# Start bytes of split weights and activations in their SBUF buffers, and two instead of three attention scratch buffers

## The chip, the cores and the metric

The kernel runs on one core of one Trainium2 chip. The metric is the device time of one execution in microseconds (us), as a median over runs. Engines are named as in the profile: PE is TensorE's matmul, PEld its weight load, DVE is VectorE, ACT is ScalarE, POOL is GpSimd, and SP issues DMAs.

## The reference

One decoder layer on 256 tokens of width 2048, all in float32:

```python
h = rmsnorm(x, ln1)
proj = h @ w_in                                   # 2048 x 6144
dq, dk, dv, sq, sk, sv = split(proj)              # six blocks of 1024 columns
diff_out = rmsnorm(differential_attention(rotary(dq), rotary(dk), dv, lam), diff_head_norm) * (1 - lam_init)
sb_out = rmsnorm(stick_breaking_attention(sq, sk, sv), sb_head_norm)
x = x + concat(diff_out, sb_out) @ w_out          # 2048 x 2048
h = rmsnorm(x, ln2)
x = x + square(relu(h @ w_mlp_in)) @ w_mlp_out    # 2048 x 8192, 8192 x 2048
return rmsnorm(x, ln_f)
```

## The kernel before

**Three passes.** Each large product is made of three passes in float32r, a 4-byte type: a value is split into H, its float32r rounding, and L, the rest, and x.w is taken as xH.wH + xH.wL + xL.wH, summed in PSUM.

**The weight stream.** Weights come by DMA in chunks of 512 rows by 512 columns (`w`, 1 MB). A chunk is used in two jobs of `HK` = 2 contraction tiles each. For a job ACT rounds half a chunk to `wh` (L214), DVE subtracts and writes `wl` (L217), both 128 x 1024 elements, which is 4,096 bytes in each partition, and PE multiplies. The conversions run 3 jobs ahead of PE, 5 in the MLP. `wh` and `wl` lie in the pool `spool`, 4 buffers each. In the MLP part every third job takes its pair from another pool, `mlp_split`, with 2 buffers each.

**The two shapes of product.** `products_acc` (L258, L259, L260) keeps activations stationary and streams weights: a matmul of 512 columns for each of xH.wH, xH.wL, xL.wH, and 12 to a job. It serves the projections dq, dk, dv, sv (`acc_..`), the output projection (`oacc`) and the second MLP product (`ma`). `products_T` (L272, L274) keeps weights stationary and streams activations: one matmul of 512 columns with wH against [xH | xL], one of 256 columns with wL against xH, 8 such pairs to a job. It serves sq, sk (`acc_sq`, `acc_sk`) and the first MLP product (`ia`). Every matmul loads a stationary operand of 128 columns (512 bytes a partition) ahead of it. Both operands are read from SBUF.

**Activations.** Split activations lie in the pool `apool` under one tag, `act`: 16 buffers of 4,096 bytes, in turn `xs`, `mixT`, `xs2` and `aT`, each [2 contraction tiles][H, L][256 tokens].

**Where the tiles begin.** In the program as built, the four `wh` buffers begin at byte 69,600 of each partition and every 4,096 after it, the `wl` buffers at 85,984, the `act` buffers at 102,368, the `mlp_split` buffers at 209,504. So all operands of these matmuls begin at 96 modulo 128. Take as *distance* the start of the stationary operand that is loaded for the next matmul minus the start of the present matmul's moving operand, modulo 512: with weights from `spool` it is 0 throughout, with weights from `mlp_split` it is 384 (L258 to L260) or 128 (L272, L274). 2,961 of the 3,920 matmuls of 512 float32r columns have distance 0.

**Attention** is written as generators that put a few instructions at a time between the jobs (`side`, `tick`). Its scratch tag `e` has three buffers: `e_d` of a differential head (L463 to L482), `t_s` and `a_s` of a pair of stick-breaking heads. PE, ACT and DVE run in the order in which the code is written; SP's loads are issued when a chunk has been converted.

Of the kernel before, what the change touches and what calls it, by code (L numbers as in the profile page):

```python
# [10 lines left out]
F32 = mybir.dt.float32  # L11
F32R = mybir.dt.float32r
BF16 = mybir.dt.bfloat16
# [3 lines left out]
PSUM = bass.MemoryType.PSUM  # L17

P = 128
S = 256  # L20
D = 2048
DFF = 4 * D
NT = S // P          # token tiles
KT = D // P          # contraction tiles of the model width
NB = 512             # columns of a weight block
CK = 4               # contraction tiles of one weight load
HK = 2               # contraction tiles of one split step
HG = 4               # heads of one column block
# [5 lines left out]
LN_IN = 2.0 ** -32                    # the Ln table ends at 2^64  # L34
LN_OUT = -16.0 * math.log(2.0)
LAM_INIT = 0.8 - 0.6 * math.exp(-0.3 * 0)
W_BUFS = 3           # weight loads in flight
S_BUFS = 4           # split steps in flight
START_ORDER = "x0 c0 x1 c1 m0 x2 c2 m1 c3 x3 m2 x4 c4 m3 c5 x5 m4 x6 c6 m5 c7 x7 m6"
WARM0, WARM1 = 5, 4  # products of zeros before and after the first transposes  # L40
AHEAD = 3            # split steps ahead of the products
# [3 lines left out]
def tile_hybrid_layer(  # L45
# [19 lines left out]
    """Every large product runs as three float32r passes: with x = H + L, H = float32r(x),  # L65
    x.w = xH.wH + xH.wL + xL.wH, all summed in float32 PSUM."""
# [9 lines left out]
    # ---------------------------------------------------------------- loads  # L76
# [16 lines left out]
    # ---------------------------------------------------------------- constants  # L93
    idle = cpool.tile([P, NB], BF16, name="idle")
# [13 lines left out]
    negtri = cpool.tile([P, P], F32, name="negtri")      # [l, j] = -1 where l >= j  # L108
# [5 lines left out]
    dmask = cpool.tile([P, 2 * P], BF16, name="dmask")   # [q, key]: key <= q is kept  # L114
    smask = cpool.tile([P, 2 * P], BF16, name="smask")   # [key, q]: key < q is kept
# [12 lines left out]
    # ---------------------------------------------------------------- helpers  # L128
    def rsqrt_mean(ss, n, width, name, r, eps=EPS, most=FMAX):
        """r = 1 / sqrt(ss / width + eps): exp(-ln/2), then one Newton step; 0 where the sum of  # L130
        squares exceeds `most` (it overflows, and the root of its inverse is 0)."""
        v = tiny.tile([P, n], F32, tag=f"v{n}", name=f"v_{name}")
        nc.vector.tensor_scalar(v, ss, 1.0 / width, eps, op0=ALU.mult, op1=ALU.add)
        nc.vector.tensor_scalar(v, v, TINY, BIG, op0=ALU.max, op1=ALU.min)
        lv = tiny.tile([P, n], F32, tag=f"lv{n}", name=f"lv_{name}")
        nc.scalar.activation(lv, v, AF.Ln, scale=LN_IN)
        r0 = tiny.tile([P, n], F32, tag=f"r0{n}", name=f"r0_{name}")
        nc.scalar.activation(r0, lv, AF.Exp, scale=-0.5, bias=lnout_c)
        a = tiny.tile([P, n], F32, tag=f"a{n}", name=f"a_{name}")
        nc.vector.scalar_tensor_tensor(a, v, -0.5, r0, op0=ALU.mult, op1=ALU.mult)  # L140
        nc.vector.tensor_tensor(a, a, r0, op=ALU.mult)
        nc.vector.scalar_tensor_tensor(a, a, 1.5, r0, op0=ALU.add, op1=ALU.mult)
        nc.vector.scalar_tensor_tensor(r, ss, most, a, op0=ALU.is_le, op1=ALU.mult)

    def split_pair(dst, ps, g, per_kt):
        """dst[:, kt, 0/1, :] = H / L of ps * g (g: one column per kt, or one for both)."""
        if per_kt:
            for j in range(HK):
                nc.scalar.activation(dst[:, j, 0, :], ps[:, j * S:(j + 1) * S], AF.Copy, scale=g[:, j:j + 1])
            for j in range(HK):  # L150
                nc.vector.scalar_tensor_tensor(dst[:, j, 1, :], ps[:, j * S:(j + 1) * S], g[:, j:j + 1],
                                               dst[:, j, 0, :].bitcast(F32),
                                               op0=ALU.mult, op1=ALU.subtract)
        else:
            pv = ps.rearrange("p (k s) -> p k s", k=HK)
            nc.scalar.activation(dst[:, :, 0, :], pv, AF.Copy, scale=g)
            nc.vector.scalar_tensor_tensor(dst[:, :, 1, :], pv, g,
                                           dst[:, :, 0, :].bitcast(F32),
                                           op0=ALU.mult, op1=ALU.subtract)

    # ---------------------------------------------------------------- weight stream
    jobs = []       # (chunk id, half, products, after)
    chunks = []     # weight views
# [7 lines left out]

    wt = {}
    sp = {}
    mlp = {"n": 0}  # pools of the second part
# [26 lines left out]
    def issue_conv():  # L201
# [10 lines left out]
        wh = ph[0].tile([P, HK, NB], F32R, tag=ph[1], name=f"wh{i}")  # L212
        for j in (range(HK) if i == 0 else (slice(0, HK),)):
            state["wh"] = nc.scalar.copy(wh[:, j], w[:, j])  # L214
        wl = pl[0].tile([P, HK, NB], F32R, tag=pl[1], name=f"wl{i}")
# [31 lines left out]
    # activations stationary, weights moving: acc[t] += act[:, tokens t].T @ w  # L247
# [15 lines left out]
    # weights stationary, activations moving: acc[i] = [wH.T @ xH | wH.T @ xL + wL.T @ xH]  # L263
# [32 lines left out]
    # ---------------------------------------------------------------- start: x -> xs  # L296
# [9 lines left out]
    def keep_clock_up(n, name):  # L306
        """products of zeros that nothing reads: the tensor engine's clock is halved until it
        has been busy for a while, and it has to wait for the first loads anyway."""
        warm = ps_acc.tile([P, NB], F32, tag="acc", name=f"warm_{name}")
        for _ in range(n):  # L310
            nc.tensor.matmul(warm, idle[:, :P], idle, start=True, stop=True)

    ghd = cpool.tile([P, 1], F32, name="ghd")
    lamc = cpool.tile([P, 2], F32, name="lamc")          # c, -lam * c with c = 1 / max(|lam|, 1)
    epsc = cpool.tile([P, 1], F32, name="epsc")          # eps * c^2
    mostc = cpool.tile([P, 1], F32, name="mostc")        # float32's largest value * c^2
# [9 lines left out]
    def x_pair(p2):  # L326
# [11 lines left out]
        xs[p2] = apool.tile([P, HK, 2, S], F32R, tag="act", name=f"xs{p2}")  # L338
# [50 lines left out]
    # ---------------------------------------------------------------- attention tasks  # L389
    grp = {}  # L390

    def prep_task(kind):
        """q / k of the differential heads: rotary, then heads transposed to [dim, token]."""
# [28 lines left out]
    def finish_pair(o, g, kt2, name, **norm):  # L422
        """per-head RMSNorm of o [q, (head, query tile), dim], transposed and split into mixT."""
# [14 lines left out]
        mixT[kt2] = apool.tile([P, HK, 2, S], F32R, tag="act", name=f"mixT{kt2}")  # L438
        split_pair(mixT[kt2], tp, g, False)

    def diff_task(gi):
        while f"dk{gi}" not in grp:
            yield
        # outputs carry the factor c, so that their squares stay in range for any lam
        qT, kT, v = grp[f"dq{gi}"], grp[f"dk{gi}"], grp[f"dv{gi}", "src"]
        for h in range(HG):
# [11 lines left out]
            nm4 = tiny.tile([P, 2, 2], F32, tag="nmax", name=f"nmax_{nm}")   # [query tile, map]  # L458
            nc.vector.tensor_reduce(nm4[:, 1, :], sc[:, :, 0:S], axis=AX.X, op=ALU.max, negate=True)
            nc.vector.tensor_reduce(nm4[:, 0, :], sc[:, :, S:S + P], axis=AX.X, op=ALU.max, negate=True)  # L460
            e = ap_.tile([P, 2, 3 * P], F32, tag="e", name=f"e_{nm}", bufs=3)
# [37 lines left out]
    def sb_task(gi):  # L499
        """scores as [key, query]: columns are (key tile 0, query tile 1), (0, 0), (1, 1)."""  # L500
# [3 lines left out]
        for hp in range(HG // 2):  # L504
# [12 lines left out]
            t = ap_.tile([P, 2, 3 * P], F32, tag="e", name=f"t_{nm}", bufs=3)  # L517
# [18 lines left out]
            a = ap_.tile([P, 2, 3 * P], F32, tag="e", name=f"a_{nm}", bufs=3)  # L536
# [11 lines left out]
    # ---------------------------------------------------------------- projections  # L548
# [3 lines left out]
    def proj_T_block(kind):  # L552
        """q / k of the stick-breaking heads, straight to [dim, token]."""
# [58 lines left out]
    # output projection: the first two column blocks stop before the last head group  # L612
# [12 lines left out]
    def x2_task(nb):  # L625
        for p2 in range(nb * 2, nb * 2 + 2):
# [7 lines left out]
            xs2[p2] = apool.tile([P, HK, 2, S], F32R, tag="act", name=f"xs2_{p2}")  # L634
# [28 lines left out]
    # ---------------------------------------------------------------- MLP stream  # L663
# [12 lines left out]
    FQ = 4                       # quarters of the hidden width  # L676
    FG = DFF // FQ // NB         # column groups of a quarter
# [4 lines left out]
    def in_group(q, g):  # L682
# [9 lines left out]
        def evacuate(i):  # L692
            nm = f"{q}{g}{i}"
            kt = g * 4 + i
            if i % 2 == 0:
                pair = apool.tile([P, HK, 2, S], F32R, tag="act", name=f"aT{nm}")
                aT[q, kt // 2] = pair
# [14 lines left out]
    def out_group(q, nb):  # L712
# [29 lines left out]
        # the last column block: all of token tile 0, then token tile 1 in two column halves  # L742
# [55 lines left out]
    def square_base(t, n):  # L798
        """the sum over all but the last piece, ready before it."""
        b = tiny.tile([P, 1], F32, tag="sqb", name=f"sqb{t}")  # L800
        nc.vector.tensor_reduce(b, ss3[:, t, 0:n], axis=AX.X, op=ALU.add)
        return b

    def finish_tokens(t, base):
        """final RMSNorm of one token tile; all but the last column block are times ln_f already."""
# [38 lines left out]
    # ---------------------------------------------------------------- run  # L844
# [31 lines left out]
def _rope_table():  # L876
    """cos | cos and -sin | sin of the first 16 dims, [token in tile, token tile, 2, 16]."""
# [36 lines left out]
```

## Time and profile before

| | |
|---|---|
| timed runs | 1139.26 and 1139.76 us, median 1139.51 us |
| profiled execution, first to last instruction | 1137.4 us |
| PE busy | 1126.2 us, 99% |
| PEld busy | 948.9 us, 83% |
| DVE busy | 659.2 us, 58% |
| ACT busy | 534.6 us, 47% |
| HBM traffic | 204.65 MB read, 182 GB/s over the span |

The profile shows one execution of its own, with a span of 1137.4 us; the timed runs are some 2 us longer, which lies ahead of its first and behind its last instruction. A busy engine is one with an instruction under way. Matmuls overlap: the shown duration of one includes the time that its results take through the array, so durations add up to more than the span, and the pace is read from start to start.

### The profile page before, as it was taken

To read this page: it belongs to the slowest core of one execution; us is meant where nothing else is said; L and a number is where in the kernel's file an instruction comes from. 1 tells how busy PE (TensorE), PEld (TensorE's weight loads), DVE (VectorE), ACT (ScalarE), POOL (GpSimd) and SP (SyncE) were. 2 spreads that over 40 slices of the span, in tenths; PEclk is the share of its full clock that TensorE was granted. 3 is DMA by queue.
4 is the path that set the end of the run, shared out by engine and by line. 5 is a ranking of instruction groups with operands and counts; after the bars stand their busy time and mean duration, and the time that the engine had idled before them with its cause. 6 is when DMAs were issued, how large, how long until landed. Compare 5 with 4: busy or idle time off the path is not lost.

```text
span 1137.4 us, 14314 instructions
## 1 busy us (share of the span) xinstructions
PE 1126.2 (99%) x5725; PEld 948.9 (83%) x5725; DVE 659.2 (58%) x929; ACT 534.6 (47%) x761; POOL 2.9 (0%) x16
## 2 busy tenths in 40 slices
PE   9999999999999999999999999999999999999996
PEld 6887888888888888888888888888888888888886
DVE  5755656656655656565455556455655545565652
ACT  5644444555554644453334444334544333454531
POOL 1000000000000000000000000000000000000000
PEclk9999999999999999999999999999999999999998
DMA  8744454444555855555565555556555566555502
GB/s 289 231 153 157 148 179 146 149 148 148 184 187 199 322 182 185 185 186 193 197 199 186 186 185 185 192 194 196 189 192 185 185 190 191 191 190 195 193 35 74
DMA packets 105207, 207.68 MB, mean 183 GB/s; under 512 B 4114, under 2 KB 5172, under 8 KB 105012
## 3 DMA queue, kind: packets, MB, share of 16 engines
q1 hardware_dynamic: 104852, 206.24, 55.0%
q8 instruction: 45, 0.74, 0.3%
q10 hardware_dynamic: 288, 0.52, 0.1%
q14 instruction: 22, 0.18, 0.0%
HBM read 204.65 MB, written 2.10 MB: 182 GB/s over the span
## 4 chain that ended last, share of the span: by engine, by line
PE 97%; DMA 2%; SPq 1%; DVE 0%; ACT 0%; issue 0%; DVEq 0%; ACTq 0%
PE ia L272 21%; PE ia L274 11%; PE ma L260 10%; PE ma L259 10%; PE ma L258 10%; PE acc_sk L272 3%; PE acc_sq L272 3%; PE oacc L260 3%; PE oacc L258 3%; PE oacc L259 3%; PE acc_sq L274 1%; PE acc_sk L274 1%; PE acc_dk L258 1%; PE acc_dk L260 1%; PE acc_sv L258 1%; PE acc_dk L259 1%
## 5 line engine op out<-in xcount | busy, mean ns | idle before, releaser
L217 DVE TENSOR_TENSOR wl<-w,wh 128x1024 fp32r<-128x1024 f32 (+1 forms) x385 | 469.1, 1222 | 396.7 <-ACT wh L214 394.8
L214 ACT CAST wh<-w 128x1024 fp32r<-128x1024 f32 (+1 forms) x385 | 401.8, 1048 | 485.3 <-PE ma L260 189.7
L272 PE MATMUL ia<-xs,wh 128*128 128x512 f32 x1024 | 357.4, 393 | 0.0
L274 PE MATMUL ia<-xs,wl 128*128 128x256 f32 x1024 | 285.7, 281 | 0.0
L272 PEld LDWEIGHTS ia<-xs,wh 128*128 128x128 f32 x1024 | 191.1, 187 | 43.0
L274 PEld LDWEIGHTS ia<-xs,wl 128*128 128x128 f32 x1024 | 193.0, 189 | 1.2
L260 PE MATMUL ma<-wh,aT 128*128 128x512 f32 x480 | 187.9, 391 | 0.0
L259 PE MATMUL ma<-wl,aT 128*128 128x512 f32 x480 | 187.8, 391 | 0.0
L258 PE MATMUL ma<-wh,aT 128*128 128x512 f32 x480 | 187.7, 391 | 0.0
L258 PEld LDWEIGHTS ma<-wh,aT 128*128 128x128 f32 x480 | 90.1, 188 | 19.9
L259 PEld LDWEIGHTS ma<-wl,aT 128*128 128x128 f32 x480 | 90.1, 188 | 19.8
L260 PEld LDWEIGHTS ma<-wh,aT 128*128 128x128 f32 x480 | 90.1, 188 | 19.8
L258 PE MATMUL oacc<-wh,mixT 128*128 128x512 f32 x128 | 50.6, 395 | 0.0
L259 PE MATMUL oacc<-wl,mixT 128*128 128x512 f32 x128 | 50.2, 392 | 0.0
L260 PE MATMUL oacc<-wh,mixT 128*128 128x512 f32 x128 | 49.9, 394 | 0.0
L272 PE MATMUL acc_sq<-xs,wh 128*128 128x512 f32 x128 | 45.3, 396 | 0.0
L272 PE MATMUL acc_sk<-xs,wh 128*128 128x512 f32 x128 | 44.9, 398 | 0.0
L274 PE MATMUL acc_sq<-xs,wl 128*128 128x256 f32 x128 | 35.8, 284 | 0.0
L274 PE MATMUL acc_sk<-xs,wl 128*128 128x256 f32 x128 | 34.4, 283 | 0.0
L260 PEld LDWEIGHTS oacc<-wh,mixT 128*128 128x128 f32 x128 | 24.0, 188 | 5.0
L258 PEld LDWEIGHTS oacc<-wh,mixT 128*128 128x128 f32 x128 | 24.1, 188 | 4.9
L259 PEld LDWEIGHTS oacc<-wl,mixT 128*128 128x128 f32 x128 | 24.1, 188 | 4.9
(225 smaller groups left out, 1128.5 us busy)
## 6 DMA issues: line engine op xcount, KB each, us to landing
w<-in_w_mlp_in_dram SPq DMA_DIRECT2D x64, 1024.0 KB, 5.4
w<-in_w_mlp_out_dram SPq DMA_DIRECT2D x64, 1024.0 KB, 5.0
w<-in_w_in_dram SPq DMA_DIRECT2D x46, 1024.0 KB, 5.2
w<-in_w_out_dram SPq DMA_DIRECT2D x16, 1024.0 KB, 5.1
w<-in_w_in_dram SPq DMA_DIRECT2D x4, 512.0 KB, 7.7
x<-in_x_dram SPq DMA_DIRECT2D x3, 512.0 KB, 10.3
lnf_t<-in_ln_f_dram SPq DMA_DIRECT2D x1, 1024.0 KB, 6.5
out_dram<-x SPq DMA_DIRECT2D x4, 256.0 KB, 3.0
```

Source lines behind the costliest of these rows:

```text
L214: state["wh"] = nc.scalar.copy(wh[:, j], w[:, j])
L217: state["wl"] = nc.vector.tensor_tensor(wl[:, j], w[:, j], wh[:, j].bitcast(F32), op=ALU.subtract)
L258: nc.tensor.matmul(acc[t], a[:, 0, st], wh[:, j, :], start=s0, stop=False)
L259: nc.tensor.matmul(acc[t], a[:, 0, st], wl[:, j, :], start=False, stop=False)
L260: state["mm"] = nc.tensor.matmul(acc[t], a[:, 1, st], wh[:, j, :], start=False, stop=s1)
L272: nc.tensor.matmul(acc[i], wh[:, j, fs], a.rearrange("p a s -> p (a s)"), start=kt == 0, stop=False, skip_group_check=True)
L274: state["mm"] = nc.tensor.matmul(acc[i][:, S:2 * S], wl[:, j, fs], a[:, 0, :], start=False, stop=kt == KT - 1, skip_group_check=True)
```

## The change

A function `place` takes the split tiles from their pools. It makes a tile longer by the largest offset of a list and uses 4,096 bytes of it from an offset that goes through the list in turn. Offsets are in elements of 4 bytes: `AT_H` for `wh` and `AT_A` for activations give 0, 32, 64, 128 bytes, `AT_L` for `wl` gives 192, 16, 96, 160 bytes. Tiles from `mlp_split` keep offset 0. The tile `idle` gets 16 more bf16 elements, which shifts all that is allocated behind it by 32 bytes. The tag `e` gets two buffers.

```diff
+AT_H = (0, 8, 16, 32)
+AT_L = (48, 4, 24, 40)
+AT_A = (0, 8, 16, 32)
...
-    idle = cpool.tile([P, NB], BF16, name="idle")
+    idle = cpool.tile([P, NB + 16], BF16, name="idle")[:, :NB]
...
+    placed = {}
+
+    def place(pool, tag, name, steps):
+
+        n = placed.get((id(pool), tag), 0)
+        placed[id(pool), tag] = n + 1
+        o = steps[n % len(steps)]
+        t = pool.tile([P, HK * NB + max(steps)], F32R, tag=tag, name=name)
+        return t[:, o:o + HK * NB]
...
-        wh = ph[0].tile([P, HK, NB], F32R, tag=ph[1], name=f"wh{i}")
+        wh = place(ph[0], ph[1], f"wh{i}", AT_A if ph[1] == "act" else AT_H if ph[0] is spool else (0,)).rearrange("p (k n) -> p k n", k=HK)
...
-        wl = pl[0].tile([P, HK, NB], F32R, tag=pl[1], name=f"wl{i}")
+        wl = place(pl[0], pl[1], f"wl{i}", AT_A if pl[1] == "act" else AT_L if pl[0] is spool else (0,)).rearrange("p (k n) -> p k n", k=HK)
...
-        xs[p2] = apool.tile([P, HK, 2, S], F32R, tag="act", name=f"xs{p2}")
+        xs[p2] = place(apool, "act", f"xs{p2}", AT_A).rearrange("p (k a s) -> p k a s", k=HK, a=2)
...
-            e = ap_.tile([P, 2, 3 * P], F32, tag="e", name=f"e_{nm}", bufs=3)
+            e = ap_.tile([P, 2, 3 * P], F32, tag="e", name=f"e_{nm}", bufs=2)
```

`mixT`, `xs2` and `aT` are taken as `xs` is, `t_s` and `a_s` have two buffers as `e` has. The other lines of the diff only drop comments.

In the program as built every engine has the same instructions in the same order, each with the same semaphores and values to wait for. What differs is where operands begin. `wh` now begins at 0, 32, 64, 0 modulo 128 in its four buffers, `wl` at 64, 80, 96, 96, `act` at 0, 32, 64, 0 in turn, `mlp_split` at 0. Of the 3,920 matmuls of 512 float32r columns 387 have distance 0; the others have one of 24 other multiples of 16. Counting those of 256 columns too, 2,743 of 5,295 have both operands at a multiple of 64 bytes, and none had before.

## Rows read from the trace of the kernel before

**Rows 1.** The page: busy time of PE, and its granted clock in 40 slices.

```profile
PE 1126.2 (99%) x5725; PEld 948.9 (83%) x5725; DVE 659.2 (58%) x929; ACT 534.6 (47%) x761; POOL 2.9 (0%) x16
...
PEclk9999999999999999999999999999999999999998
```

**Rows 2.** The page: the chain that ended last, by engine.

```profile
PE 97%; DMA 2%; SPq 1%; DVE 0%; ACT 0%; issue 0%; DVEq 0%; ACTq 0%
```

**Rows 3.** All waits of PE: for whom, us in total, times, longest.

```profile
PE warm_a L311 <- DVE three_c L105: 1.3, 1, 1.3
PE ps_g1T L299 <- DMA rows<-in_ln_dram: 0.5, 1, 0.5
PE acc_dq L259 <- DVE wl L217: 0.5, 1, 0.5
```

**Rows 4.** Groups of PE over the span: count, busy us, mean ns of one.

```profile
L272 PE MATMUL ia<-xs,wh 128*128 128x512 f32 x1024 | 357.4, 393 | 0.0
L274 PE MATMUL ia<-xs,wl 128*128 128x256 f32 x1024 | 285.7, 281 | 0.0
L260 PE MATMUL ma<-wh,aT 128*128 128x512 f32 x480 | 187.9, 391 | 0.0
...
L260 PE MATMUL oacc<-wh,mixT 128*128 128x512 f32 x128 | 49.9, 394 | 0.0
...
L274 PE MATMUL acc_sk<-xs,wl 128*128 128x256 f32 x128 | 34.4, 283 | 0.0
...
L258 PE MATMUL acc_dv<-wh,xs 128*128 128x512 f32 x64 | 25.1, 392 | 0.0
```

**Rows 5.** Timeline, 699.0 to 704.6: spool job, then mlp_split job; start us, duration us.

```profile
699.05 0.39 PE L258 MATMUL ma<-wh,aT 128*128 128x512 f32 x1
699.06 0.19 PEld L259 LDWEIGHTS ma<-wl,aT 128*128 128x128 f32 x1
699.25 1.05 ACT L214 CAST wh<-w 128x1024 fp32r<-128x1024 f32 x1 [1.69 <-PE ma L260]
...
700.34 1.23 DVE L217 TENSOR_TENSOR wl<-w,wh 128x1024 fp32r<-128x1024 f32 x1 [1.51 <-ACT wh L214]
...
701.77 0.40 PE L258 MATMUL ma<-wh,aT 128*128 128x512 f32 x1
...
704.57 0.39 PE L258 MATMUL ma<-wh,aT 128*128 128x512 f32 x1
```

**Rows 6.** Groups of PE, 699.5 to 701.4, within the spool job.

```profile
L259 PE MATMUL ma<-wl,aT 128*128 128x512 f32 x4 | 1.6, 389 | 0.0
L260 PE MATMUL ma<-wh,aT 128*128 128x512 f32 x3 | 1.2, 389 | 0.0
```

**Rows 7.** Groups of PE, 702.5 to 704.2, within the mlp_split job.

```profile
L259 PE MATMUL ma<-wl,aT 128*128 128x512 f32 x3 | 1.2, 396 | 0.0
L258 PE MATMUL ma<-wh,aT 128*128 128x512 f32 x3 | 1.2, 394 | 0.0
```

**Rows 8.** Groups of PE, 682.8 to 685.0: `ia`, weights from spool.

```profile
L272 PE MATMUL ia<-xs,wh 128*128 128x512 f32 x8 | 2.8, 391 | 0.0
L274 PE MATMUL ia<-xs,wl 128*128 128x256 f32 x7 | 2.0, 280 | 0.0
```

**Rows 9.** Groups of PE, 677.1 to 679.5: `ia`, weights from mlp_split.

```profile
L272 PE MATMUL ia<-xs,wh 128*128 128x512 f32 x8 | 2.8, 393 | 0.0
L274 PE MATMUL ia<-xs,wl 128*128 128x256 f32 x7 | 2.0, 282 | 0.0
```

**Rows 10.** Groups of PE, 671.5 to 673.9: `ia`, weights from spool again.

```profile
L272 PE MATMUL ia<-xs,wh 128*128 128x512 f32 x8 | 2.9, 399 | 0.0
L274 PE MATMUL ia<-xs,wl 128*128 128x256 f32 x7 | 2.0, 281 | 0.0
```

**Rows 11.** Groups of PE, 224.30 to 224.32: a matmul of bf16.

```profile
L509 PE MATMUL sc_s<-smask,identb 128*128 128x256 bf16 x1 | 0.3, 272 | 0.0
```

**Rows 12.** The page: the conversions, with the idle time before them and its releaser.

```profile
L217 DVE TENSOR_TENSOR wl<-w,wh 128x1024 fp32r<-128x1024 f32 (+1 forms) x385 | 469.1, 1222 | 396.7 <-ACT wh L214 394.8
L214 ACT CAST wh<-w 128x1024 fp32r<-128x1024 f32 (+1 forms) x385 | 401.8, 1048 | 485.3 <-PE ma L260 189.7
```

More of the change, by code (lines that the diff above doesn't have):

```diff
@@ L437, in finish_pair @@
         yield
-        mixT[kt2] = apool.tile([P, HK, 2, S], F32R, tag="act", name=f"mixT{kt2}")
+        mixT[kt2] = place(apool, "act", f"mixT{kt2}", AT_A).rearrange("p (k a s) -> p k a s", k=HK, a=2)
         split_pair(mixT[kt2], tp, g, False)
@@ L516, in sb_task @@
             z = sc[:, :, :3 * P]
-            t = ap_.tile([P, 2, 3 * P], F32, tag="e", name=f"t_{nm}", bufs=3)
+            t = ap_.tile([P, 2, 3 * P], F32, tag="e", name=f"t_{nm}", bufs=2)
             nc.scalar.activation(t, z, AF.Abs)
@@ L535, in sb_task @@
             yield
-            a = ap_.tile([P, 2, 3 * P], F32, tag="e", name=f"a_{nm}", bufs=3)
+            a = ap_.tile([P, 2, 3 * P], F32, tag="e", name=f"a_{nm}", bufs=2)
             nc.scalar.activation(a, z, AF.Exp)
@@ L633, in x2_task @@
             yield
-            xs2[p2] = apool.tile([P, HK, 2, S], F32R, tag="act", name=f"xs2_{p2}")
+            xs2[p2] = place(apool, "act", f"xs2_{p2}", AT_A).rearrange("p (k a s) -> p k a s", k=HK, a=2)
             split_pair(xs2[p2], tp, gT[2][:, p2 * HK:(p2 + 1) * HK], True)
@@ L695, in evacuate @@
             if i % 2 == 0:
-                pair = apool.tile([P, HK, 2, S], F32R, tag="act", name=f"aT{nm}")
+                pair = place(apool, "act", f"aT{nm}", AT_A).rearrange("p (k a s) -> p k a s", k=HK, a=2)
                 aT[q, kt // 2] = pair
```

## The prediction

> **What bounds the kernel now.** I read the page first, then PE's waits, then the pace of single matmuls.
>
> PE is busy for 1126.2 of 1137.4 us, at the full granted clock in every slice but the last [rows 1], and the chain that ended last lies on PE for 97% [rows 2]. PE waits for another engine three times in the whole execution, 2.3 us together, all of it at the start [rows 3]. So nothing that feeds PE sets the time. Its matmuls follow each other without a gap, and only their own pace can move the end.
>
> The pace is read from start to start. In the spool job the first matmul of one job starts at 699.05 and that of the next at 701.77; 12 matmuls lie between, so one takes 2.72 / 12 = 0.227 us. The mlp_split job that follows takes 704.57 - 701.77 = 2.80, or 0.233 us each [rows 5]. The shown durations are 389 ns in the first [rows 6] and 394 to 396 in the second [rows 7]: a duration is the pace and some 162 ns behind it, so a difference in durations is a difference in pace, in ns, and I use durations from here.
>
> The products make up nearly all. L258 to L260 are 3 x (480 + 128 + 4 x 64) = 2,592 matmuls at about 391, L272 1,280 at about 393, L274 1,280 at about 281 [rows 4], where one row stands for the like groups. Less 162 each, that is 2,592 x 0.229 + 1,280 x (0.231 + 0.119) = 1,042 us of the span. One ns on each of these 5,152 is 5.2 us.
>
> **What hides what.** The spool job runs at 389 both while ACT writes the next `wh` (from 699.25) and while DVE writes the next `wl` (from 700.34) [rows 5, 6]. So the writes of other engines don't show in PE's pace, and the differences between the jobs come from the two reads of PE itself. The weight load of the next matmul starts 0.01 us after the present matmul [rows 5], so both read SBUF at once.
>
> **The change part by part.**
>
> *The attention tag.* Every engine has the same rows and the same waits with two buffers, so no instruction waits for a buffer that it did not wait for before. Cost 0. What hides it is not slack but that the third buffer's release was never the last thing waited for; nothing is queued behind a new wait.
>
> *The conversions.* ACT and DVE write and read at other bytes: 385 of 1,048 ns and 385 of 1,222 ns [rows 12]. DVE stood idle for 396.7 us and ACT for 485.3 us ahead of these groups, mostly for each other and for PE to free a buffer [rows 12]. Were they 10% slower (40 and 47 us spread over the whole), this idle time would take it. Cost 0; without that cover it would be those 47 us. The DMAs into `w` are the same in number and size. The shift of `idle` moves products that nothing reads, at the start. Cost 0.
>
> *PE's operands.* This is all that is left. The trace shows three things on it.
> First, the place of the operands does matter: same instruction, same clock, 389 at distance 0 and 394 to 396 at distance 384 [rows 6, 7]. With weights stationary it is 391 and 280 at distance 0 [rows 8], 393 and 282 at distance 128 [rows 9].
> Second, distance 0 is not all: another stretch at distance 0 runs at 399 and 281 [rows 10], so a fast repeating pattern can be lost and stay lost for a job.
> Third, a matmul of 256 columns can be shorter than any of these: one of bf16 operands, half the bytes, took 272 [rows 11], 8 below the 280 of the fast pattern.
>
> One rule speaks against any effect. The Trainium skill, SBUF — State Buffer, section "Who interferes with whom", gives PE two independent read ports, one for the moving operand and one for weight loads, and states that PE and ACT never wait on anyone. By that the start bytes would change nothing and the sum would be 0; rows 6 and 7 disagree with it, 389 against 396. The Trainium skill, TensorE: Matmul & The Clock Gate, section on 56 ns against 53.3, gives N / 2.4 + 2.5 ns from start to start, 215.7 at 512 columns; the trace has 227 to 233; taken at that page's pace throughout, the sum would as an estimate be some 67 us less, and no row here reaches it.
>
> No row shows the new places, since all operands began at 96 modulo 128 and only distances 0, 128 and 384 occur in these products. So I bound the cost from both sides.
>
> Low end: every matmul 8 ns under the fast pattern, as the bf16 row is: 381 for 512 columns (389 - 8) and 272 for 256. Against the means that is 10 x 2,592 + 12 x 1,280 + 9 x 1,280 ns = 25.9 + 15.4 + 11.5 = 52.8 us less: 1086.7.
> High end: every matmul as in the slow stretches, 396 [rows 7], 399 and 282 [rows 9, 10]: 5 x 2,592 + 6 x 1,280 + 1 x 1,280 ns = 13.0 + 7.7 + 1.3 = 22.0 us more: 1161.5.
>
> The value between: 2,743 of 5,295 matmuls, 52%, have both operands at a multiple of 64 bytes after the change. Theirs are places of a kind that no row has, and a run of 2,048 bytes that begins there touches 32 pieces of 64 bytes where one from 96 modulo 128 touches 33. For these I take half of the low end. The other 48% lose distance 0 without such a start; they are nearest to rows 7, 9 and 10, and as half of the matmuls before them may hold a fast pattern I take half of the high end. That is -52.8 / 2 x 0.52 + 22.0 / 2 x 0.48 = -13.7 + 5.3 = -8.4 us. The sum is made on the profiled span, 1137.4 to 1129.0; the median of the runs shown is 2.1 above the span, so the time is 1131.1, say 1131 us, 0.7% less. That half is a choice, not a reading.
>
> **The rivals.**
>
> *The fast pattern is lost and nothing comes for it.* Two thirds of the jobs take their weights from spool and most of them repeat one pattern at 389 or at 391 and 280. It rests on distance 0, which 2,961 of 3,920 have now and 387 after. If distance and not the multiple of 64 decides, all jobs run as those of mlp_split: 395 for L258 to L260, 393 and 282 for the others: 4 x 2,592 + 0 + 1 x 1,280 ns = 11.7 us more, 1151; with the slow stretch throughout, 1161.5. Its place is the spool jobs of PE; it decides from the point where the mean for 512 columns passes 392. For it: every distance but 0 that these products have is slower. Against it: these are two distances of the 31 others. It is the rival on the other side.
>
> *The operands keep out of each other's way nearly everywhere.* Then most of the low end is taken, two thirds of it: -35 us, 1104. For it: row 11. Against it: the offsets of `wh` and `act` are drawn from one list, mlp_split gets none, so all combinations meet and some will be bad; and no matmul of float32r in rows 6 to 10 is near 381. It begins to count as faster by over 2% when 43% of the low end is reached.
>
> *The change does nothing that shows.* The places of SBUF matter in another way than by start bytes modulo 512, as between pools; then 1139.5. The rule of the Trainium skill on PE's ports, above, gives the same. Against it: rows 7 and 9 differ from rows 6 and 8 by nothing but the pool and with it the start.
>
> **How the numbers follow.** My forecast, a mixture with a small gain, gets 0.45, the lost pattern 0.25, the clear gain 0.22, no effect 0.08. The predicted time is 1131. Its own range is 1117 to 1146. For 8 in 10 the low side must reach past the 1104 of the clear gain and leaves out less than half of that case, 0.10; I put it at 1100. The high side takes in the 1151 and most of the way to 1161.5: 1157, which leaves out 0.08. Two per cent, 22.8 us, is taken as what a measurement of this kernel can tell from no change: below 1116.7 lies the clear gain and a little of the forecast, 0.23; above 1162.3 only what goes past the slow stretch, 0.07; between them 0.70.
>
> **What would show it.** The page should name the same counts, PE at 99%, and no new wait of PE behind 10 us. The groups should have L258 to L260 at about 389 to 390 in the mean, L272 at 390 to 391 and L274 at 279 to 280, with spool jobs no longer of one value but with both shorter and longer ones than 389. A mean above 392 speaks for the lost pattern, one under 385 for the clear gain, 391, 393 and 281 as before for no effect. Attention groups should keep their durations. I would be wrong in kind if ACT or DVE got so much slower that PE waited for `wl` in the middle of the span, or if the granted clock changed.

## The result, and the profile after

The changed kernel takes 1147.19 us (1146.54 and 1147.84), against 1139.51 before: a ratio of 1.0064, 95% interval 1.0045 to 1.0083. That is inside the range on record and on the other side of its forecast: 7.7 us slower where 8.4 us less was expected. The profiled spans are 1144.8 and 1137.4 us, 7.4 apart.

The page of the changed kernel, its lines on PE, on the clock, on the chain and on the conversions. L230 and L227 are L217 and L214 of before.

```profile
PE 1133.9 (99%) x5725; PEld 949.1 (83%) x5725; DVE 659.7 (58%) x929; ACT 534.4 (47%) x761; POOL 2.9 (0%) x16
...
PEclk9999999999999999999999999999999999999999
...
PE 99%; DMA 0%; DVE 0%; SPq 0%; ACT 0%; issue 0%; DVEq 0%; ACTq 0%
...
L230 DVE TENSOR_TENSOR wl<-w,wh 128x1024 fp32r<-128x1024 f32 (+1 forms) x385 | 469.4, 1222 | 402.9 <-ACT wh L227 401.1
L227 ACT CAST wh<-w 128x1024 fp32r<-128x1024 f32 (+1 forms) x385 | 401.1, 1046 | 492.5 <-PE ma L273 193.5
```

All waits of PE in the changed kernel (for whom, us in total, times, longest):

```profile
PE warm_a L324 <- DVE three_c L108: 1.3, 1, 1.3
PE ps_g1T L312 <- DMA rows<-in_ln_dram: 0.5, 1, 0.5
PE xtp L347 <- DMA x<-in_x_dram: 0.4, 1, 0.4
```

Counts and clock are those of before [rows 1], PE holds 99% of the chain and not 97% [rows 2], and its three waits, all at the start, come to 2.2 us and not 2.3 [rows 3]. The conversions take what they took and stand idle 6 to 7 us longer ahead of their groups [rows 12]. PE alone is longer: 1133.9 us busy, not 1126.2. So the difference is in the pace of its matmuls.

PE's groups in the changed kernel over the span (count, busy us, mean ns of one). L271 to L273 are L258 to L260 of before, L285 and L287 are L272 and L274:

```profile
L285 PE MATMUL ia<-xs,wh 128*128 128x512 f32 x1024 | 358.5, 395 | 0.0
L287 PE MATMUL ia<-xs,wl 128*128 128x256 f32 x1024 | 285.8, 281 | 0.0
L271 PE MATMUL ma<-wh,aT 128*128 128x512 f32 x480 | 189.2, 394 | 0.0
L273 PE MATMUL ma<-wh,aT 128*128 128x512 f32 x480 | 188.8, 393 | 0.0
L272 PE MATMUL ma<-wl,aT 128*128 128x512 f32 x480 | 188.8, 393 | 0.0
```

Against [rows 4] `ma` went from 391 to 393 or 394, L285 from 393 to 395, L287 stayed at 281. Busy time says it more finely. A 395 ns L285 still runs when the next one starts, so these overlap and the group's busy time is the time in which one pair of L285 and L287 follows another: 358.5 us / 1,024 = 350.1 ns a pair, against 357.4 / 1,024 = 349.0 before. I call that the *pair pace* below.

Summed over the rows of this view, busy time grew by 3.5 us in the `ma` groups, 0.8 in `oacc`, 1.9 in the twelve `acc_d..` and `acc_sv` groups, 1.1 in L285 of `ia` and 0.3 in L285 of `acc_sq` and `acc_sk`. That is 7.6 us, and the span grew by 7.4. Every large product is slower by a little, and the rest of PE's groups together are not.

### The profile page after: what moved, and what is told of

Read it like the earlier page. It is cut to its first block, busy times and chain, and to the rows that moved or that the text cites. A ratio compares the mean times of both kernels' runs of the same rounds, so it can differ in the third digit from the quotient of the medians.

```text
span 1144.8 us, 14314 instructions
## 1 busy us (share of the span) xinstructions
PE 1133.9 (99%) x5725; PEld 949.1 (83%) x5725; DVE 659.7 (58%) x929; ACT 534.4 (47%) x761; POOL 2.9 (0%) x16
## 4 chain that ended last, share of the span: by engine, by line
PE 99%; DMA 0%; DVE 0%; SPq 0%; ACT 0%; issue 0%; DVEq 0%; ACTq 0%
PE ia L285 21%; PE ia L287 11%; PE ma L271 10%; PE ma L272 10%; PE ma L273 10%; PE acc_sk L285 3%; PE oacc L271 3%; PE acc_sq L285 3%; PE oacc L273 3%; PE oacc L272 3%; PE acc_sq L287 1%; PE acc_dq L271 1%; PE acc_dk L271 1%; PE acc_sk L287 1%; PE acc_dk L273 1%; PE acc_dq L272 1%
## 5 line engine op out<-in xcount | busy, mean ns | idle before, releaser
L230 DVE TENSOR_TENSOR wl<-w,wh 128x1024 fp32r<-128x1024 f32 (+1 forms) x385 | 469.4, 1222 | 402.9 <-ACT wh L227 401.1
L227 ACT CAST wh<-w 128x1024 fp32r<-128x1024 f32 (+1 forms) x385 | 401.1, 1046 | 492.5 <-PE ma L273 193.5
L285 PE MATMUL ia<-xs,wh 128*128 128x512 f32 x1024 | 358.5, 395 | 0.0
L287 PE MATMUL ia<-xs,wl 128*128 128x256 f32 x1024 | 285.8, 281 | 0.0
L285 PEld LDWEIGHTS ia<-xs,wh 128*128 128x128 f32 x1024 | 191.5, 188 | 43.8
L287 PEld LDWEIGHTS ia<-xs,wl 128*128 128x128 f32 x1024 | 192.8, 188 | 1.3
L271 PE MATMUL ma<-wh,aT 128*128 128x512 f32 x480 | 189.2, 394 | 0.0
L273 PE MATMUL ma<-wh,aT 128*128 128x512 f32 x480 | 188.8, 393 | 0.0
L272 PE MATMUL ma<-wl,aT 128*128 128x512 f32 x480 | 188.8, 393 | 0.0
L273 PEld LDWEIGHTS ma<-wh,aT 128*128 128x128 f32 x480 | 90.1, 188 | 21.3
L271 PEld LDWEIGHTS ma<-wh,aT 128*128 128x128 f32 x480 | 90.1, 188 | 21.0
L272 PEld LDWEIGHTS ma<-wl,aT 128*128 128x128 f32 x480 | 90.2, 188 | 20.8
L271 PE MATMUL oacc<-wh,mixT 128*128 128x512 f32 x128 | 50.9, 398 | 0.0
L272 PE MATMUL oacc<-wl,mixT 128*128 128x512 f32 x128 | 50.5, 394 | 0.0
L273 PE MATMUL oacc<-wh,mixT 128*128 128x512 f32 x128 | 50.1, 396 | 0.0
L285 PE MATMUL acc_sq<-xs,wh 128*128 128x512 f32 x128 | 45.5, 397 | 0.0
L285 PE MATMUL acc_sk<-xs,wh 128*128 128x512 f32 x128 | 45.0, 398 | 0.0
L287 PE MATMUL acc_sq<-xs,wl 128*128 128x256 f32 x128 | 35.9, 284 | 0.0
L287 PE MATMUL acc_sk<-xs,wl 128*128 128x256 f32 x128 | 34.5, 284 | 0.0
L273 PEld LDWEIGHTS oacc<-wh,mixT 128*128 128x128 f32 x128 | 24.0, 188 | 5.3
L271 PEld LDWEIGHTS oacc<-wh,mixT 128*128 128x128 f32 x128 | 24.1, 188 | 5.2
L272 PEld LDWEIGHTS oacc<-wl,mixT 128*128 128x128 f32 x128 | 24.1, 188 | 5.1
```

What stands on the lines that cost most here:

```text
L230: state["wl"] = nc.vector.tensor_tensor(wl[:, j], w[:, j], wh[:, j].bitcast(F32), op=ALU.subtract)
L271: nc.tensor.matmul(acc[t], a[:, 0, st], wh[:, j, :], start=s0, stop=False)
L272: nc.tensor.matmul(acc[t], a[:, 0, st], wl[:, j, :], start=False, stop=False)
L273: state["mm"] = nc.tensor.matmul(acc[t], a[:, 1, st], wh[:, j, :], start=False, stop=s1)
L285: nc.tensor.matmul(acc[i], wh[:, j, fs], a.rearrange("p a s -> p (a s)"), start=kt == 0, stop=False, skip_group_check=True)
L287: state["mm"] = nc.tensor.matmul(acc[i][:, S:2 * S], wl[:, j, fs], a[:, 0, :], start=False, stop=kt == KT - 1, skip_group_check=True)
```

## The experiments

Each run was timed against the kernel before on the same chip. Distances are given modulo 256 from here on; why that is enough is shown by the run at 256. Line numbers move with each edit. Whatever the number, a row of `ma`, `oacc`, `acc_d..` or `acc_sv` with 512 columns is of L258 to L260 of before, `ia<-xs,wh` is L272 and `ia<-xs,wl` is L274, and the text calls them so.

**The tag alone.** The kernel before, with two buffers in place of three for the tag `e`:

```diff
-... tag="e", name=f"e_{nm}", bufs=3)
+... tag="e", name=f"e_{nm}", bufs=2)
```

(`t_s` and `a_s` likewise.)

> The kernel before with two buffers for the attention tag and no other edit. Every theory expects no effect, 1139.5 us within 0.5, since no instruction gets a new wait and the operands of the large products begin where they began. If it were 1147, the whole loss would be the tag's and the start bytes would be innocent.

1139.75 us, ratio 1.0000 [0.9991, 1.0009], span 1137.3. The tag costs nothing, as forecast.

**All starts moved by 32 bytes.** The kernel before with the longer `idle` only. All operands of the large products then begin at a multiple of 128 bytes, and the distances between them are as before:

```diff
-    idle = cpool.tile([P, NB], BF16, name="idle")
+    idle = cpool.tile([P, NB + 16], BF16, name="idle")[:, :NB]
```

> The kernel before with all tiles behind the constant tile moved by 32 bytes, so that the operands of the large products begin at 0 modulo 128 and not at 96, and every distance stays. Distance theory (the pace hangs on the distance between the two reads): 1139.5 within 1, matmuls of L258 to L260 at 389 ns in spool jobs. Alignment theory (the pace hangs on where an operand begins modulo 64 or 128): another time than before, 1147 if the loss is from the new starts alone, since here all operands are moved; the gain on which the prediction counted for starts at a multiple of 64 would give about 1113.

1139.25 us, ratio 0.9997 [0.9988, 1.0006]. PE's groups over the span:

```profile
L272 PE MATMUL ia<-xs,wh 128*128 128x512 f32 x1024 | 357.4, 393 | 0.0
L274 PE MATMUL ia<-xs,wl 128*128 128x256 f32 x1024 | 285.7, 281 | 0.0
L260 PE MATMUL ma<-wh,aT 128*128 128x512 f32 x480 | 187.9, 391 | 0.0
```

These are [rows 4] to the last digit. Moving both operands from 96 to 0 modulo 128 changes nothing. This removes the ground of the forecast's gain.

**Only the longer tiles.** The changed kernel with all offsets 0 and the tile lengths kept, so buffers follow each other after 4,224 or 4,288 bytes, not 4,096:

```diff
-AT_H = (0, 8, 16, 32)
-AT_L = (48, 4, 24, 40)
-AT_A = (0, 8, 16, 32)
+AT_H = (0, 0, 0, 0)
+AT_L = (0, 0, 0, 0)
+AT_A = (0, 0, 0, 0)
...
-        t = pool.tile([P, HK * NB + max(steps)], F32R, tag=tag, name=name)
+        t = pool.tile([P, HK * NB + (0 if len(steps) == 1 else 48 if tag == "wl" else 32)], F32R, tag=tag, name=name)
```

> The changed kernel with all offsets 0 but tiles as long as in the change, so that buffers lie 4,224 and 4,288 bytes apart and distances are multiples of 64, spread evenly, a quarter or less of them 0. Distance theory: as the changed kernel, 1147 within 2, since distance 0 is lost just as well. A theory that the offsets of 16, 32, 96 or 160 bytes within a tile cost: 1139.5.

1144.70 us, ratio 1.0045 [1.0032, 1.0058]. PE's groups over the span:

```profile
L285 PE MATMUL ia<-xs,wh 128*128 128x512 f32 x1024 | 356.6, 393 | 0.0
...
L273 PE MATMUL ma<-wh,aT 128*128 128x512 f32 x480 | 188.7, 393 | 0.0
```

Every operand begins at a multiple of 64 bytes here, yet `ma` stands at 393 as in the changed kernel. The time is just below the 1147 within 2 of the distance theory and well above 1139.5. Some two thirds of the loss (0.45 of 0.64%) comes with the length of the tiles, whatever the offsets are: in the program as built the length alone leaves 1,203 of the 3,920 matmuls of 512 float32r columns at distance 0 modulo 256. The changed kernel leaves 676.

This kernel has both kinds of job side by side. By its addresses 20 of the 120 jobs of `ma` have distance 0 throughout and 40 have 128. A job at 128 (window 691.9 to 694.3 us) and, from its fifth matmul on, a job at 0 (698.4 to 699.6 us):

```profile
L272 PE MATMUL ma<-wl,aT 128*128 128x512 f32 x4 | 1.6, 395 | 0.0
L273 PE MATMUL ma<-wh,aT 128*128 128x512 f32 x4 | 1.6, 394 | 0.0
```

```profile
L272 PE MATMUL ma<-wl,aT 128*128 128x512 f32 x2 | 0.8, 389 | 0.0
L273 PE MATMUL ma<-wh,aT 128*128 128x512 f32 x2 | 0.8, 389 | 0.0
```

So a job that still has distance 0 comes back to 389 with the longer tiles too.

**Distance 0 everywhere.** The kernel before with 384 bytes ahead of the pool `mlp_split`, so its jobs have distance 0 too:

```diff
+    spad = ctx.enter_context(tc.tile_pool(name="spad", bufs=1))
+    nc.gpsimd.memset(spad.tile([P, 96], F32, name="spad_t"), 0.0)
```

> The kernel before with 384 bytes ahead of the mlp_split pool, so that its jobs have distance 0 too. Distance theory: those jobs go from 395 to 389 ns (some 530 matmuls x 5.5 ns = 2.9 us), L274 from 283 to 280 on 344 (0.9 us), and the first matmuls of the spool jobs behind them, that were slow, as well (0.7 and 1.3 us): about 1134, below both kernels. Alignment theory: nothing changes modulo 128, so 1139.5. A theory that pools as such differ: 1139.5.

1137.57 us, ratio 0.9981 [0.9972, 0.9989]. PE's groups over the span:

```profile
L272 PE MATMUL ia<-xs,wh 128*128 128x512 f32 x1024 | 358.9, 397 | 0.0
L274 PE MATMUL ia<-xs,wl 128*128 128x256 f32 x1024 | 284.5, 280 | 0.0
L258 PE MATMUL ma<-wh,aT 128*128 128x512 f32 x480 | 186.8, 389 | 0.0
```

`ma` is at 389 in all jobs: the pace of [rows 6], now without the mlp_split jobs of [rows 7]. `ia` did not follow. Its pair pace became 358.9 / 1,024 = 350.5 ns. The same kernel's `ia` in two windows, 430 to 432.5 and 600 to 602.5 us:

```profile
L272 PE MATMUL ia<-xs,wh 128*128 128x512 f32 x8 | 2.8, 391 | 0.0
L274 PE MATMUL ia<-xs,wl 128*128 128x256 f32 x9 | 2.5, 280 | 0.0
```

```profile
L272 PE MATMUL ia<-xs,wh 128*128 128x512 f32 x8 | 2.9, 399 | 0.0
L274 PE MATMUL ia<-xs,wl 128*128 128x256 f32 x8 | 2.2, 281 | 0.0
```

At distance 0 L272 and L274 repeat one of several patterns, as in [rows 8] and [rows 10], and hold it for long. In the kernel before, every third job has another distance [rows 9], and the pattern behind it can be another one; here nothing breaks it, and by the mean of 397 the slow one holds most of the time. That the other jobs break the pattern is a reading that no run tests. So the run misses the time expected of it by the `ia` part, and confirms the `ma` part.

**The same distance everywhere, but not 0.** The kernel of the last run with X bytes ahead of the activation pool and 384 - X ahead of `mlp_split`, for X = 32, 64, 128 and 256 (each kernel has the numbers themselves):

```diff
+    gap = ctx.enter_context(tc.tile_pool(name="gap", bufs=1))
+    nc.gpsimd.memset(gap.tile([P, X // 4], F32, name="gap_t"), 0.0)
...
+    nc.gpsimd.memset(spad.tile([P, (384 - X) // 4], F32, name="spad_t"), 0.0)
```

They ask whether 0 counts, or only that the distance never changes.

> The kernel of split_at_zero (all weights at one place modulo 512) with the activation pool moved by 32 bytes: distance 32 in L258 to L260 and 480 in L272 and L274, the same for every matmul. Theory that distance 0 itself is the good one: all matmuls lose it, 392 to 395 ns in place of 389, about 1147 to 1155. Theory that constancy is what counts (a pattern can repeat at any distance, and the change lost it by mixing): as split_at_zero, 1137.6 within 2.

> As the run before, with 64 bytes: distance 64 in L258 to L260, 448 in L272 and L274. Distance 0 itself: 1147 to 1155. Constancy: 1137.6 within 2. A third possibility, that some other distance is better than 0: below 1136.

> As before, with 128 bytes: distance 128 in L258 to L260, 384 in L272 and L274. Distance 0 itself: as the mlp_split jobs of the kernel before in every job, 395 ns, and L274 at 282: about 1151 to 1158. Constancy: 1137.6 within 2.

> As before, with 256 bytes: distance 256 in all of them, as far from 0 as can be modulo 512. Distance 0 itself: 1147 to 1158. Constancy: 1137.6 within 2. A theory that the two reads hinder each other when they are near modulo 512 would have this as the best of all, below 1130.

PE's groups over the span, of X = 32, of X = 64 and of X = 256:

```profile
L274 PE MATMUL ia<-xs,wh 128*128 128x512 f32 x1024 | 354.8, 390 | 0.0
...
L260 PE MATMUL ma<-wh,aT 128*128 128x512 f32 x480 | 189.8, 396 | 0.0
```

```profile
L274 PE MATMUL ia<-xs,wh 128*128 128x512 f32 x1024 | 359.8, 395 | 0.0
...
L260 PE MATMUL ma<-wh,aT 128*128 128x512 f32 x480 | 189.9, 396 | 0.0
```

```profile
L274 PE MATMUL ia<-xs,wh 128*128 128x512 f32 x1024 | 358.9, 397 | 0.0
...
L260 PE MATMUL ma<-wh,aT 128*128 128x512 f32 x480 | 186.8, 389 | 0.0
```

The four take 1148.19, 1153.67, 1151.09 and 1137.41 us: ratios 1.0076 [1.0059, 1.0092], 1.0119 [1.0104, 1.0134], 1.0098 [1.0083, 1.0113] and 0.9974 [0.9964, 0.9983]. A constant distance does not help: 32, 64 and 128 are no faster than the changed kernel with its mixed ones (1.0064). 256 gives what 0 gives, in these rows to the digit. So it is the distance modulo 256 that counts, as far as this pair shows, and for L258 to L260 0 is special. `ia` goes another way: at X = 32 it is faster than at 0, 354.8 us against 358.9.

**Other offsets of the stationary and the moving weights.** Weights are the moving operand in `products_acc` and the stationary one in `products_T`. In the next three kernels a weight tile is 256 bytes longer and begins at one offset for the one and at another for the other; `mlp_split` has the place of `spool` modulo 256, and the tag has two buffers. The offsets are in elements of 4 bytes, 0 and 56 in the first, 8 and 8 in the second, 60 and 60 in the third:

```diff
+AT_ACC, AT_T = 0, 56
...
+            t = pool.tile([P, HK * NB + 64], F32R, tag=tag, name=name)[:, at[i]:at[i] + HK * NB]
...
```

> Two scratch buffers for the tag, weight tiles 256 bytes longer, and a weight tile begins 224 bytes later when it is stationary (L272, L274) than when it is moving: distance 0 modulo 256 in L258 to L260, 224 (that is 32 short of 256) in L272 and L274. Distance theory with the map of the four runs before: L258 to L260 at 389 as in split_at_zero, L272 and L274 at 390 and 282 as in all_32_apart, so 4 ns less for each of 1,280 pairs than split_at_zero, 1132 to 1133, below all so far. If the order of jobs or the pools make the pattern, 1137 or more.

> As the run before, with 32 bytes for both: distance 224 in L258 to L260 and 32 in L272 and L274, the mirror of all_32_apart. If it counts how far the two reads are apart and not which is ahead: as all_32_apart, L258 to L260 at 395, L272 and L274 at 390 and 282, 1148. If the sign counts (stationary 32 short of the moving operand is good, 32 past it bad): L258 to L260 at 390 to 391 and L272 and L274 slower than 390 and 282, about 1141 to 1145.

> As acc_0_T_224, with 240 bytes for both: distance 16 in L258 to L260 and 240 in L272 and L274. If the pace falls off smoothly from 0: L258 to L260 at 391 to 393, L272 and L274 near 390 and 281, about 1140. If reads are taken in pieces of 32 bytes or more, 16 does as 0 or as 32: 389 or 395 in L258 to L260, 1133 or 1148.

1133.85, 1149.36 and 1154.98 us: ratios 0.9943 [0.9930, 0.9955], 1.0082 [1.0068, 1.0096] and 1.0136 [1.0120, 1.0151]. PE's groups over the span, of the first and of the last:

```profile
L284 PE MATMUL ia<-xs,wh 128*128 128x512 f32 x1024 | 354.8, 390 | 0.0
L286 PE MATMUL ia<-xs,wl 128*128 128x256 f32 x1024 | 286.8, 282 | 0.0
L270 PE MATMUL ma<-wh,aT 128*128 128x512 f32 x480 | 186.8, 389 | 0.0
```

```profile
L284 PE MATMUL ia<-xs,wh 128*128 128x512 f32 x1024 | 355.2, 393 | 0.0
...
L271 PE MATMUL ma<-wl,aT 128*128 128x512 f32 x480 | 192.1, 400 | 0.0
```

The first was put together from the runs above, `ma` at 0 and `ia` at the distance of the run with X = 32, and beats both kernels. It is 5.8 us under the kernel before. Summed as in the result, busy time moved by -3.2 in `ma`, -0.3 in `oacc`, +1.9 in the other projections with stationary activations, -2.6 in L272 of `ia` and -0.5 in that of `acc_sq` and `acc_sk`: -4.7 us, and the span by -4.8.

The +1.9 is not a matter of places. It lies in `acc_dq`, the first product, and there at the start. PE's groups of 9.2 to 12.6 us in this run and in the kernel before (a row of each):

```profile
L271 PE MATMUL acc_dq<-wl,xs 128*128 128x512 f32 x3 | 1.9, 628 | 0.0
```

```profile
L259 PE MATMUL acc_dq<-wl,xs 128*128 128x512 f32 x5 | 2.0, 393 | 0.0
```

PE had waited 1.2 us for `x` just before; why its matmuls are slow behind that is not shown (the granted clock of the stretch is given as 1.00). `acc_dq` takes 76.1 us in the kernel before, 77.0 in that of distance 0 everywhere and 78.1 here, all at distance 0 modulo 256, so a difference of 2 us between two profiled executions can be their start alone. Without the +1.9 the groups are 6.6 us shorter.

The second run gives what X = 32 gave (1.0082 and 1.0076), so it does not matter which of the two reads is ahead by 32 bytes. The last came out as none of its theories: the loss does not fall off towards 0, and 16 bytes is the worst distance of all that were tried for `ma`. All runs of one distance together:

| distance of L258 to L260 | `ma`, mean ns | distance of L272, L274 | pair pace of `ia`, ns | ratio of time |
|---|---|---|---|---|
| 0 | 389 | 224 | 354.8 / 1,024 = 346.5 | 0.9943 |
| 0 (256 bytes) | 389 | 0 | 350.5 | 0.9974 |
| 0 | 389 | 0 | 350.5 | 0.9981 |
| 32 | 396 | 224 | 346.5 | 1.0076 |
| 224 | 395 | 32 | 346.4 | 1.0082 |
| 128 | 395 | 128 | 350.5 | 1.0098 |
| 64 | 396 | 192 | 351.4 | 1.0119 |
| 16 | 400 | 240 | 346.9 | 1.0136 |

**Shorter weight loads.** Does the load of the next stationary operand take reads from the matmul that runs? Then loads of 64 columns, half the bytes, should cut the price of a bad distance. First in two of three matmuls at distance 0 (of the sums for the second half of each token tile, two of three passes are left out; L260 is cut in the same way, but for the last of a sum):

```diff
-nc.tensor.matmul(acc[t], a[:, 0, st], wl[:, j, :], start=False, stop=False)
+nc.tensor.matmul(acc[t][0:HALF], a[:, 0, t * P:t * P + HALF], wl[:, j, :], start=False, stop=False)
...
```

> The kernel of split_at_zero, but the matmuls of L259 and L260 (all but the last L260 of a sum) load 64 stationary columns in place of 128 and write 64 rows: the second half of the tokens of each tile lacks two of the three passes. Places and moving operands stay. Theory of two reads at once (the weight load of the next matmul slows the present one's moving operand): the matmul ahead of a half load, L258 and L259, gets shorter than 389 ns, by some 5 (half of the 11 that lie above 512 columns at 2.4 GHz, plus 2), L260, which stands ahead of the full load of L258, stays at 389: about 1,700 x 5 ns = 9 us less than 1137.5. Theory that the own load counts: L259 and L260 get shorter, L258 not. Theory that the moving operand's place alone counts: all stay at 389, 1137.5.

1142.65 us, ratio 1.0027 [1.0017, 1.0038]. PE's groups over the span:

```profile
L260 PE MATMUL ma<-wl,aT 128*64 128x512 f32 x480 | 188.8, 393 | 0.0
L262 PE MATMUL ma<-wh,aT 128*64 128x512 f32 x480 | 187.6, 391 | 0.0
L259 PE MATMUL ma<-wh,aT 128*128 128x512 f32 x480 | 187.3, 390 | 0.0
```

No theory had expected this: the loads of 64 columns are shorter, and the matmuls around them are longer by 1 to 4 ns. Since a mixture of lengths might break a pattern, all of L258 to L260 but the first and last of a sum then got short loads, at distance 0 and at 64:

```diff
+n = P if s0 else HALF
+nc.tensor.matmul(acc[t][0:n], a[:, 0, t * P:t * P + n], wh[:, j, :], start=s0, stop=False)
...
```

> The kernel of split_at_zero with 64 stationary columns in all of L258 to L260 but the first and the last of a sum; the second half of the tokens of each tile lacks most of its products. Distance 0, every load half as long. If the bytes of the weight load cost time: below 389 ns, some 384, and about 1125 to 1130. If what cost in half_load was only that long and short loads alternate: the pattern is back, 389 as in split_at_zero, 1137.6. If half loads as such lose it: 390 to 392 as in half_load, 1142.

> The same on the kernel of all_64_apart, distance 64 in L258 to L260. If the bytes of the load cost time: the 6 ns that distance 64 costs with full loads are halved, 392, about 1145. If the distance costs whatever the load's length: 395 and 1153.7.

1142.05 and 1150.18 us, ratios 1.0019 [1.0010, 1.0028] and 1.0084 [1.0067, 1.0101]. The first is what its third theory had. PE's groups over the span, at distance 0 and at 64:

```profile
L261 PE MATMUL ma<-wl,aT 128*64 128x512 f32 x480 | 188.8, 393 | 0.0
L260 PE MATMUL ma<-wh,aT 128*64 128x512 f32 (+1 forms) x480 | 188.5, 393 | 0.0
L263 PE MATMUL ma<-wh,aT 128*64 128x512 f32 x480 | 187.3, 390 | 0.0
```

```profile
L263 PE MATMUL ma<-wl,aT 128*64 128x512 f32 x480 | 190.6, 397 | 0.0
L262 PE MATMUL ma<-wh,aT 128*64 128x512 f32 (+1 forms) x480 | 188.2, 392 | 0.0
L265 PE MATMUL ma<-wh,aT 128*64 128x512 f32 x480 | 187.8, 391 | 0.0
```

The three rows give (188.8 + 188.5 + 187.3) / 1,440 = 392.1 ns and 566.6 / 1,440 = 393.5, so distance 64 costs 1.4 ns with short loads, where it costs 6 to 7 with full ones (389 and 396). That a shorter load makes the distance matter less fits a collision between load and matmul. That it loses the 389 at distance 0 does not. A theory in which only the bytes of the load count has fallen. The short loads did take less time, 134 to 139 ns in place of 188. But these runs change more than the load: the matmul behind it writes 64 rows in place of 128, and they do not tell which of the two lost the 389.

## Why the prediction was wrong

**What bounds the kernel: right.** PE alone, at an unchanged clock, without a wait behind the start. All of the 7.4 us is pace.

**The tag and the conversions at 0: right.** Shown by the run of the tag alone, and by 1222 and 1046 ns for the conversions.

**That the relation of PE's two operands sets the pace: right in kind.** Runs whose instructions are the same but for a memset or two, and whose operands lie elsewhere, take 389 to 400 ns for `ma` and span 2% of the time.

**The step that failed is the term "for these I take half of the low end", the -13.7 us for matmuls with both operands at a multiple of 64 bytes.** It rested on a count of the 64-byte pieces that a run of 2,048 bytes touches. Moving all operands to a multiple of 128 bytes changed nothing (0.9997), and the kernel with only the longer tiles has all operands at a multiple of 64 and is 0.45% slower. So the runs leave nothing of the term: such a start makes no difference here. The bf16 matmul that the low end came from [rows 11] was no neighbour: the lowest mean of a large product over the span is, in any run, 389 for 512 columns and 279 for 256, not 381 and 272.

**The other term, +5.3 us for the rest, was mis-sized by its share.** It was put on 48% of the matmuls. With the gain at nothing, the loss falls on nearly all that left distance 0: half of the high end on all of them would have been +11.0, and +7.4 came.

**The rival of the lost pattern is what happened.** It was priced at +11.7 us with the paces of the mlp_split jobs, and +7.4 came. The pairs of L272 and L274 fit it: they rose by 1.1 ns, where it had 1. What it had too high is L258 to L260: their groups grew by 6.2 us, where it had 10.4. The `ma` of the changed kernel is at 393 and 394, not at the 395 of those jobs. That its distances are mixed may be the reason, but the prices of the table don't add up to it: every distance but 0 that was tried by itself gives 395 or more, and some 80 of its 1,440 matmuls of `ma` have distance 0. Why a mixture costs less stays open. The rival's point of decision, a mean above 392 for 512 columns, showed the right side. Against it I had put that two slow distances are few of 31. The four further ones that were tried for L258 to L260 (16, 32, 64 and 224) are slow as well.

**What stays open** is why distance 0 modulo 256 is the good one for L258 to L260, and which load it is that counts, a matmul's own or the next. In the runs of one distance the two are the same. The kernel before has six places where they differ. PE's groups of 235.80 to 235.82 us, two matmuls of one projection:

```profile
L259 PE MATMUL acc_sv<-wl,xs 128*128 128x512 f32 x1 | 0.4, 397 | 0.0
L258 PE MATMUL acc_sv<-wh,xs 128*128 128x512 f32 x1 | 0.4, 389 | 0.0
```

Both have their own stationary operand at distance 0; behind this L259 the load of another tile, `negtri_r`, starts 0.01 us after it, at distance 32. It takes 397, and so do four of the other five matmuls with this load behind them; the sixth takes 395. This points to the next load. In the second of the three kernels with other offsets the same load is at distance 0 and the matmul's own at 224. PE's groups of 320.44 to 320.46 us there:

```profile
L271 PE MATMUL acc_sv<-wl,xs 128*128 128x512 f32 x1 | 0.4, 398 | 0.0
```

The six take 393 to 398, so a single next load at 0 does not bring 389. Nor does the first row prove the case: the matmul behind it is of another product, of 384 columns, and that alone may break a pattern. The Trainium skill, SBUF — State Buffer, section "Who interferes with whom", gives PE two independent ports for moving operand and weight load. The runs disagree as far as this goes: nothing on PE but the places of its operands differs between 389 and 400. Whether the two reads meet in SBUF, or the start of each matmul slips against its load, no run here tells, and the short loads speak against the simple form of the first. Nor is it known what chooses among the patterns of L272 and L274 at distance 0.

## What to carry to other kernels

Where PE is the bound and streams float32r operands back to back, compare the durations of one matmul form across buffers: a difference of some ns between buffers that hold data of the same kind can be the place of the operands, and padding that looks harmless (a longer tile, another pool ahead) shifts it. Measure a few distances between the stationary and the moving operand for each form of product by itself, since the best one differs: here 0 for moving weights and 32 bytes either way for stationary ones, worth 0.6% against the kernel before and 1.2% (0.9943 / 1.0064) against the changed one. And give a benefit that no row shows no value of its own: the only rows on other places spoke for a loss.

## What the runs showed of the hardware that was not expected

- With activations stationary, the duration of a matmul of 512 float32r columns depends on the distance of its two operands modulo 256 bytes: 389 ns at 0 and at 256, 400 at 16, 395 or 396 at 32, 64, 128 and 224. It is no smooth function, and the place nearest to 0 that was tried is the worst. Where the two begin together, at 96 or at 0 modulo 128, has no part in it (0.9997).
- The two shapes of product want opposite things. For the pairs with stationary weights 16 and 32 bytes off are the best of the constant distances that were tried (346.4 to 346.9 ns a pair), and 0 gives 350.5 with stretches of several paces.
- Weight loads of half the columns took 134 to 139 ns in place of 188, and the matmuls around them were longer at distance 0, 392 ns in the mean and not 389.
